# A sixth seven-product pair in the first halves of the down-projection's four-group parts, and more block sums kept in HBM

## The chip, the cores and the metric

The kernel runs on one core of a Trainium2 chip. The metric is the device time of one execution in microseconds (us); the time of a version is the median of its runs. TensorE multiplies matrices and accumulates in PSUM (eight banks of 128 x 512 float32). VectorE and ScalarE work element by element, GpSimd (POOL) does a little and issues some transfers, SyncE (SP) issues most transfers between HBM and the on-chip memory SBUF. The engines run side by side, each through its own instructions in their order, and wait for each other by semaphores.

## The reference

A decoder trunk of two layers on 256 tokens with a width of 2048. The first layer mixes tokens by a gated spatial product, the second by latent attention; both add attention into 256 memory tokens. Each layer ends with a gated feed-forward part with a causal convolution over three tokens. All is float32. The feed-forward part is what the change is about:

```python
def conv_ffn(h, w_up, cw, cb, w_down):
    S = h.shape[1]
    a = h @ w_up                                   # 256 x 2048 by 2048 x 11264
    ap = jnp.pad(a, ((0, 0), (CONV_W - 1, 0), (0, 0)))
    c = sum(ap[:, k:k + S] * cw[k] for k in range(CONV_W)) + cb
    gate, val = c[..., :D_FF], c[..., D_FF:]       # D_FF = 5632
    return (jax.nn.silu(gate) * val) @ w_down      # 256 x 5632 by 5632 x 2048
```

`out = rmsnorm(x + conv_ffn(rmsnorm(x)))` closes the second layer; the first hands `x` on to the next.

## The kernel before, in words

**Precision.** Each float32 operand is split in a rounded high half and the rest (`whi` and `wlo` for weights). A product is three matmuls: high by high, high by low, low by high. ScalarE writes the high half (L718 in the down-projection, L127 in the up-projection), VectorE the low half (L719, L128). Weights come through `raw` (four buffers of 512 KB) or `gate` (two) and go into `whi` (four) and `wlo` (five), so that loads and splits run ahead of TensorE.

**Parts.** The 11 groups of 512 hidden columns are worked in three parts of 4, 4 and 3 groups (`FF_GROUPS`). In a part, each group has an up-projection for the gate and one for the value, of eight chunks of weights each (`gemm_fm`). Each chunk is 24 matmuls of 256 columns. After the last chunk of an up-projection its four blocks of 128 hidden columns leave PSUM: `conv` multiplies by the row norm (L246, tile `a`, two buffers), then makes the three-tap convolution (L967 on ScalarE, L968 and L969 on VectorE, tile `c`, three buffers); `ev` multiplies by the gate (L989, or L996 and L1000) and splits the result as an operand of the down-projection (L254 and L255, or L1007 and L1008). Small jobs are hung on the chunks (`hooks`, by number of the chunk).

**The down-projection.** After its groups a part multiplies its 8 (or 6) pairs of 128-row blocks with the matching rows of `w_ffn_down`, first for the left 1024 output columns (half 0), then for the right (half 1). This is `down_phase`. A plain pair takes 2 blocks x 2 token halves x 2 column halves x 3 = 24 matmuls of 512 columns. A fast pair takes seven products of sums of blocks instead of eight (Strassen's way), 7 x 3 = 21 matmuls, into the accumulators e00, e01, e10 and m1, m5, m6, m7. For that the operand is kept in seven or eight quarters (`parts7`, made at L996 to L1008), and the weights need two tiles of sums beside the blocks themselves (`t13`, `t24`, four additions of 128 x 512). After the last fast pair of a half the four m accumulators are copied to `staged`; they are added to the result in the next part (`combine`).

**Where the sums come from.** There are three ways. Early sums (`FF_EARLY`): loaded and added in the last group's up-projections, for pairs 2 and 6 in a tile that shares its place (`xT`) with `staged`, for pair 5 in `xs` (two buffers). Stored sums (`FF_STORED`): long before, a hook loads 1 MB of the weights, adds, and POOL stores the sums in HBM (L792); the half loads them back into `xs`, or, for the one case named in `FF_STAGED`, into the free part of `staged`. Late sums (`late_sums`, L808): added on the spot. `FF_STORED` gives for each part (-1 is the output projection before) the hook's number, counted in chunks from the part's start, and the case (part, pair, half).

**Order.** `FF_FAST` gives for each half which pairs are fast and the order of all pairs. Loads on SP and splits on ScalarE and VectorE keep the program's order in `down_phase` (`behind`). Other instructions are put in order by the framework: each engine takes, by a simulated clock, the first instruction in program order that is ready. In half 0 of a four-group part the order is 0, 1, 5, 2, 7, 3, 6, 4, of which 2, 3, 4, 5, 6 are fast; pair 3's sums are stored, pair 4's late. The blocks of group g are 4g to 4g + 3 within the part, so pairs 6 and 7 come from the last group. What does not fit into the tile `h` goes to four `places` (tiles hx0 to hx3; other names in the last layer); a profile writes all of these as hhx.

Of the kernel before, what the change touches and what calls it, by code (L numbers as in the profile page):

```python
# [8 lines left out]
F32 = mybir.dt.float32  # L9
# [4 lines left out]
ALU = mybir.AluOpType  # L14
AX = mybir.AxisListType

P = 128
D = 2048
# [14 lines left out]
FF_GROUPS = (4, 4, 3)  # L33
FF_EARLY = {4: (2, 6, 5), 3: (1, 2, 4)}
FF_STORED = {
# [4 lines left out]
}  # L40
FF_STAGED = {4: (5, 1), 3: (5, 0)}
FF_FAST = {
    4: (((2, 3, 4, 6, 5), (0, 1, 5, 2, 7, 3, 6, 4)), ((2, 3, 4, 6, 5), (0, 2, 1, 3, 5, 4, 7, 6))),
    3: (((1, 2, 4, 5), (0, 3, 1, 2, 4, 5)), ((), (0, 1, 2, 3, 4, 5))),
}

# [35 lines left out]
class Kernel:  # L82
# [180 lines left out]
    def rstd(self, out, sums, n, pool, tag):  # L263
        nc = self.nc
        shape = list(out.shape)
        v = self.tmp(pool, shape, tag + "v", 1)
        r = self.tmp(pool, shape, tag + "r", 1)
        q = self.tmp(pool, shape, tag + "q", 1)
        nc.vector.tensor_scalar(v, sums, 1.0 / n, EPS, ALU.mult, ALU.add)
        nc.scalar.activation(r, v, AF.Sqrt)  # L270
        nc.vector.reciprocal(r, r)
        nc.vector.tensor_tensor(q, r, r, ALU.mult)
        nc.vector.scalar_tensor_tensor(q, q, -0.5, v, ALU.mult, ALU.mult)
        nc.vector.scalar_tensor_tensor(out, q, 1.5, r, ALU.add, ALU.mult)
# [487 lines left out]
    def stored_sums(self, l, case, pool):  # L762
        part, k, ph = case
        dn = self.t["w_ffn_down"][l][sum(FF_GROUPS[:part]) * 512 :]
        order = mybir.DependencyInfo(mybir.DependencyClass.NoSync, mybir.DependencyReason.DATA)
        add = lambda o, a, b: self.tc.keep_in_program_order(self.nc.vector.tensor_tensor(o, a, b, ALU.add))  # L766
        left, right, c = slice(0, 512), slice(512, 1024), 1024 * ph
        held = []

        def load(out, in_):  # L770
            ins = self.nc.sync.dma_start(out=out, in_=in_)
            self.tc.add_manual_dep(ins.ins, self.last_raw, order, reason="behind")

        def loads():
            held.extend(self.tmp(pool(), [P, 1024], "xs", 2) for _ in range(2))
            t13, t24 = held
            x, y = (dn[(2 * k + i) * P : (2 * k + i + 1) * P, c : c + 1024] for i in range(2))
            load(out=t13, in_=x)
            load(out=t24[:, left], in_=y[:, right])
            load(out=t24[:, right], in_=y[:, left])  # L780

        def adds():
            t13, t24 = held
            add(t13[:, left], t13[:, left], t13[:, right])
            add(t13[:, right], t13[:, right], t24[:, left])
            add(t24[:, left], t24[:, left], t13[:, left])
            add(t24[:, right], t24[:, right], t24[:, left])

        def stores():
            kept = self.stored[l, *case] = self.dram.tile([P, 2, 1024], F32, name=self.uid("stored"))  # L790
            for i in range(2):
                self.nc.gpsimd.dma_start(out=kept[:, i], in_=held[i])  # L792

        return loads, adds, stores

    def storing(self, l, part, pool):
        hooks = {}
        for n, case in FF_STORED[part].items():
            loads, adds, stores = self.stored_sums(l, case, pool)
            for m, f in (n, loads), (n + 5, adds), (n + 8, stores):  # L800
                hooks.setdefault(m // 8, {}).setdefault(m % 8, []).append(f)
        return hooks

    def late_sums(self, raws, pool):
# [29 lines left out]
    def down_phase(self, dn, col, order, fast, lhs, rhs, pool, fp, between, evict, finish, late=0, late_gains=None, hooks={}, sums={}, stored={}):  # L834
# [3 lines left out]
        left, right = slice(0, 512), slice(512, 1024)  # L838
# [4 lines left out]
        total = dict(todo)  # L843
# [15 lines left out]
        kept = []  # L859
        last_fast = [k for k in order if k in fast][-1:]  # L860
        for n, k in enumerate(order):
            raws = []
            for i in range(2):
                if n % 3 == (2 if col else 1) and n > 1:
                    raw = self.tmp(fp, [P, 1024], "gate", 2)
                else:
                    raw = self.wp.tile([P, 1024], F32, tag="raw", name=self.uid("raw"), bufs=4)
                raws.append(raw)
            kept_sums = stored.get((k, col // 1024))
            load = lambda o, a: self.behind(self.nc.sync.dma_start(out=o, in_=a))  # L870
            row = lambda i, c: load(raws[i][:, :c], dn[(2 * k + i) * P : (2 * k + i + 1) * P, col : col + c])
            blocks = sums.get(k)
            if kept_sums is None:
                row(0, 1024 if blocks is None else 512)
                row(1, 1024)
            else:
                if (k, col // 1024) == FF_STAGED[len(order) // 2]:
                    tile = self.tokens.staged[:, 1].rearrange("p m c -> p (m c)")
                    blocks = [tile[:, i * 1024 : (i + 1) * 1024] for i in range(2)]
                else:  # L880
                    blocks = [self.tmp(pool, [P, 1024], "xs", 2) for _ in range(2)]
                row(1, 1024)
                for i in (1, 0):
                    load(blocks[i], kept_sums[:, i])
                row(0, 512)
            if k in fast and blocks is None:
                blocks = self.late_sums(raws, pool)
            if late_gains is not None and 2 <= n:
                late_gains(n - 2)
            if k in fast:  # L890
                names7 = "e00", "e01", "e10", "m6", "m5", "m7", "m1"
                for name, q, w in zip(names7, (1, 6, 2, 5, 4, 3, 0), self.fast_pair(raws, blocks)):
                    three(name, rhs(k, q), w)
                if k in last_fast:
                    between([acc[m] for m in names[0]])
            else:
                ws = self.plain_pair(raws)
                if n < len(order) - late:
                    for tb in range(2):
                        for half in range(2):  # L900
                            plain(k, ws, tb, half)
                else:
                    kept.append((k, ws))
            for f in hooks.get(n, ()):
                f()
# [6 lines left out]
        with self.tc.manual_schedule(engines={ET.PE, ET.DVE, ET.Activation}):  # L912
# [9 lines left out]
            k, ws = kept[-1]  # L922
# [510 lines left out]


class Tokens:
    places = ("hx0", 0), ("hx1", 0), ("hx2", 0), ("hx3", 0)

    def __init__(self, kernel, pool):
        self.k, self.nc, self.pool = kernel, kernel.nc, pool
# [40 lines left out]
    def between(self, accs):  # L1480
        for i, acc in enumerate(accs):
            self.nc.scalar.activation(self.staged[:, self.ph, i, :], acc, AF.Copy)
        self.waiting.append(self.ph)
# [90 lines left out]


class Last(Tokens):
    places = ("kT1", 32), ("mv1", 0), ("hx", 0), ("hx3", 0)

    def __init__(self, kernel, pool):
        super().__init__(kernel, pool)  # L1580
# [19 lines left out]
    def evict(self, tb, half, acc, piece=None, meanwhile=lambda: None):  # L1600
        k, nc, xt, sums = self.k, self.nc, self.xt, self.sums
        c0, n = (0, 512) if piece is None else (256 * piece, 256)
        j, o = self.added(tb, half, acc, c0, n)
        c = slice(j * 512 + c0, j * 512 + c0 + n)
        if not self.last:
            return
        one = lambda x: x[:, tb : tb + 1]
        part, r, q, v, gb = self.part, self.r, self.q, self.v, self.gb
        junk = k.tmp(self.pool, [P, 512], "fjunk", 2)
        if piece == 1:  # L1610
            nc.vector.tensor_tensor_reduce(
                out=junk[:, :n], in0=o, in1=o, scale=-0.5 / D, scalar=one(part), op0=ALU.mult, op1=ALU.add, accum_out=one(v)
            )
        else:
            nc.scalar.activation(junk[:, :n], o, AF.Square, accum_out=sums[:, tb, j : j + 1])
        if piece == 0:
            self.added(tb, half, acc, 256, 256)
        meanwhile()
        if j < 3 and not (tb and j == 2):
            nc.vector.tensor_tensor(o, o, gb[:, c], ALU.mult)  # L1620
# [4 lines left out]
            if tb:  # L1625
                nc.vector.tensor_tensor(o, o, gb[:, c], ALU.mult)
        if j == 3:
            if piece != 1:
                total = one(part) if piece == 0 else one(v)
                nc.vector.tensor_scalar(total, sums[:, tb, 3:4], -0.5 / D, one(part), ALU.mult, ALU.add)  # L1630
            if piece == 0:
                return
            nc.scalar.activation(one(r), one(v), AF.Sqrt, scale=-2.0)
            nc.vector.reciprocal(one(r), one(r))
            nc.vector.scalar_tensor_tensor(one(q), one(r), one(r), one(v), ALU.mult, ALU.mult)
            nc.vector.scalar_tensor_tensor(one(r), one(q), 1.5, one(r), ALU.add, ALU.mult)
# [36 lines left out]
```

## Time and profile before

| | |
|---|---|
| median of 3 runs | 2022.09 us (2021.52 to 2022.26) |
| the profiled execution | 2022.45 us, its span 2020.7 us |
| TensorE busy | 2010.5 us (99%) |
| VectorE, ScalarE busy | 1665.6 us (82%), 1184.9 us (59%) |
| down-projection of the first part, layer 0 | 528.11 to 608.70 us |
| moved by DMA | 463.27 MB, 229 GB/s |

A row of a timeline has the start, the duration, the engine, the line of the kernel, the operation, the tiles written and read, the shape and the count; in brackets stands the idle time before it and what ended it. A row of windows has the stretch, its length, the busy time of TensorE, of its weight loads, of VectorE, ScalarE and POOL, the granted clock (1.00 is full), the share of the DMA engines and GB/s. Matmuls are pipelined, and each is shown longer than the distance to the next; so one reads distances between starts. The execution's time is longer than the span by what lies around the program.

### The profile page before, as it was taken

How to read it: one execution, taken by the hardware profiler on the slowest of the kernel's cores; microseconds unless marked ns; L12 is line 12 of the kernel's file. 1: busy time of each engine (PE TensorE's matmuls, PEld its weight loads, DVE VectorE, ACT ScalarE, POOL GpSimd, SP SyncE). 2: the span in 40 equal slices, each digit the busy share in tenths (PEclk: the TensorE clock that was granted, in tenths of full speed). 3: DMA queues.
4: the chain of work that ended last, by engine and by line, in shares of the span. 5: the costliest groups of instructions: out<-in, count | busy, mean ns of one | idle time of the engine just before them, and what ended most of it. 6: DMA issues, size and time to landing. Idle time of an engine off the chain costs nothing.

```text
span 2020.7 us, 38415 instructions
## 1 busy us (share of the span) xinstructions
PE 2010.5 (99%) x15098; PEld 1905.3 (94%) x15098; DVE 1665.6 (82%) x2519; ACT 1184.9 (59%) x1687; POOL 129.1 (6%) x205
## 2 busy tenths in 40 slices
PE   9999999999999999999999999999999999999998
PEld 8989999999989999899989999999988999889996
DVE  6866767788898788988988787778889878898897
ACT  6754744555665556655576675455566555665565
POOL 0000013100000000000002142400000000000000
PEclk9999999999999999999999999999999999999999
DMA  8775567888668786678566636788867878667865
GB/s 256 232 217 180 166 217 254 232 293 276 210 235 266 246 275 211 233 234 261 185 224 187 183 113 203 235 242 288 275 206 237 273 237 275 206 235 233 275 187 179
DMA packets 269897, 463.27 MB, mean 229 GB/s; under 512 B 77774, under 2 KB 85268, under 8 KB 269716
## 3 DMA queue, kind: packets, MB, share of 16 engines
q1 hardware_dynamic: 264340, 441.40, 68.6%
q0 software_dynamic: 5184, 18.88, 2.6%
q8 instruction: 118, 1.93, 0.4%
q14 instruction: 63, 0.52, 0.1%
q10 hardware_dynamic: 192, 0.54, 0.1%
HBM read 435.06 MB, written 20.97 MB: 226 GB/s over the span
## 4 chain that ended last, share of the span: by engine, by line
PE 98%; DVE 1%; ACT 1%; DMA 0%; issue 0%; SPq 0%; ACTq 0%; DVEq 0%
PE ps L166 22%; PE ps L167 22%; PE ps L169 22%; PE ps L850 7%; PE ps L851 7%; PE ps L852 7%; PE ps L198 2%; PE ps L199 2%; PE ps L200 2%; PE ps L533 1%; DMA raw<-in_w_ffn_down 0%; PE ps L613 0%; PE ps L612 0%; PE ps L611 0%; PE ps L415 0%; PE ps L1324 0%
## 5 line engine op out<-in xcount | busy, mean ns | idle before, releaser
L127 ACT ACTIVATE whi<-raw 128x1024 fp32r<-128x1024 f32 x484 | 513.7, 1062 | 528.7 <-PE ps L167 387.3
L128 DVE TENSOR_TENSOR wlo<-raw,whi 128x1024 fp32r<-128x1024 f32 x484 | 597.1, 1238 | 204.2 <-ACT whi L127 200.6
L166 PE MATMUL ps<-xhl,whi 128*128 128x256 f32 x3264 | 763.3, 277 | 0.0
L167 PE MATMUL ps<-xhl,whi 128*128 128x256 f32 x3264 | 761.6, 276 | 0.0
L167 PEld LDWEIGHTS ps<-xhl,whi 128*128 128x128 f32 x3264 | 612.8, 188 | 0.4
L166 PEld LDWEIGHTS ps<-xhl,whi 128*128 128x128 f32 x3264 | 612.8, 188 | 0.4
L169 PE MATMUL ps<-xhl,wlo 128*128 128x256 f32 x3264 | 438.0, 276 | 0.0
L169 PEld LDWEIGHTS ps<-xhl,wlo 128*128 128x128 f32 x3264 | 401.1, 188 | 0.0
L851 PE MATMUL ps<-wlo,h 128*128 128x512 f32 x354 | 137.1, 388 | 0.1
L719 DVE TENSOR_TENSOR wlo<-raw,whi 128x1024 fp32r<-128x1024 f32 x94 | 113.9, 1219 | 20.9 <-ACT whi L718 20.0
L718 ACT ACTIVATE whi<-raw 128x1024 fp32r<-128x1024 f32 x94 | 98.4, 1054 | 52.7 <-PE ps L167 32.2
L166 PE MATMUL ps<-mainhl,whi 128*128 128x256 f32 x512 | 119.7, 277 | 0.0
L167 PE MATMUL ps<-mainhl,whi 128*128 128x256 f32 x512 | 119.3, 276 | 0.0
L852 PE MATMUL ps<-whi,h 128*128 128x512 f32 (+1 forms) x306 | 118.4, 388 | 0.0
L967 ACT ACTIVATE c<-a,cT 128x256 f32<-128x256 f32 x176 | 99.0, 591 | 29.4 <-DVE a L246 28.4
L850 PE MATMUL ps<-whi,h 128*128 128x512 f32 x354 | 108.3, 389 | 0.0
L167 PEld LDWEIGHTS ps<-mainhl,whi 128*128 128x128 f32 x512 | 96.0, 188 | 0.0
L166 PEld LDWEIGHTS ps<-mainhl,whi 128*128 128x128 f32 x512 | 95.9, 188 | 0.0
L792 POOL DMA_DIRECT2D stored<-xs x36 | 19.8, 550 | 1158.9 <-DVE xs L766 985.1
L718 ACT ACTIVATE whi<-xs 128x1024 fp32r<-128x1024 f32 x60 | 62.7, 1058 | 47.6 <-DVE xs L808 23.7
L133 DVE SCALAR_TENSOR_TENSOR wlo<-raw,gT,whi 128x512 fp32r<-128x512 f32 x96 | 71.0, 779 | 21.3 <-ACT whi L132 21.2
L852 PE MATMUL ps<-whi,hhx 128*128 128x512 f32 x216 | 84.0, 389 | 0.0
(401 smaller groups left out, 3131.6 us busy)
## 6 DMA issues: line engine op xcount, KB each, us to landing
raw<-in_w_ffn_up SPq DMA_DIRECT2D x352, 512.0 KB, 4.6
raw<-in_w_ffn_down SPq DMA_DIRECT2D x102, 512.0 KB, 5.8
raw<-in_w_out SPq DMA_DIRECT2D x64, 512.0 KB, 4.4
raw<-in_w_in_a SPq DMA_DIRECT2D x56, 512.0 KB, 4.4
gate<-in_w_ffn_down SPq DMA_DIRECT2D x38, 512.0 KB, 5.0
stored<-xs POOLq DMA_DIRECT2D x36, 512.0 KB, 5.3
raw<-in_w_mem_kv SPq DMA_DIRECT2D x31, 512.0 KB, 3.6
xs<-in_w_ffn_down SPq DMA_DIRECT2D x24, 512.0 KB, 6.5
```

Of the source, the lines that this page charges most:

```text
L127: nc.scalar.activation(hi[:, :n], raw[:, :n], AF.Copy)
L128: nc.vector.tensor_tensor(lo[:, :n], raw[:, :n], hi[:, :n].bitcast(F32), ALU.subtract)
L133: nc.vector.scalar_tensor_tensor(lo[:, s], raw[:, s], gains[k], hi[:, s].bitcast(F32), ALU.mult, ALU.subtract)
L166: mm(acc[:, :S], wh, x[:, :S], start=first, stop=False)
L167: mm(acc[:, :S], wh, x[:, S:], start=False, stop=False)
L169: mm(acc[:, :S], wl, x[:, :S], start=False, stop=last)
L718: self.behind(self.nc.scalar.activation(hi, w, AF.Copy))
L719: self.behind(self.nc.vector.tensor_tensor(lo, w, hi.bitcast(F32), ALU.subtract))
L850: mm(o, xh, wh, start=start, stop=False)
L851: mm(o, xh, wl, start=False, stop=False)
L852: mm(o, xl, wh, start=False, stop=stop)
L967: nc.scalar.activation(c, a, AF.Identity, scale=w(2), bias=w(3))
```

## The change

In half 0 of the four-group parts pair 1 becomes the sixth fast pair, and pairs 4 and 1 have their sums stored ahead, as pair 3 has. That makes 13 stored cases in a layer where there were 9, 12 of them for four-group parts. The order of that half becomes 0, 7, 2, 6, 5, 3, 4, 1. Stored cases now start every eight chunks, and each is hung on the chunks in five pieces (two loads, the additions, two stores) at 0, 1, 5, 6 and 7 chunks from its start, where there were three pieces at 0, 5 and 8. Pair 3's stored sums come back into one half of `staged` and pair 1's into the other, pair 4's into `xs`. A fifth place is added for operands; to make room the row norm uses the `sq` buffers for two of its tiles. At the very end, the sum of squares of the last quarter is put together after the last addition and not before it.

```diff
 FF_STORED = {
-    -1: {8: (0, 2, 1), 20: (0, 5, 1)},
-    0: {17: (0, 3, 0), 28: (0, 4, 1), 39: (1, 3, 0)},
-    1: {8: (1, 2, 1), 22: (1, 5, 1), 36: (1, 4, 1)},
+    -1: {8: (0, 2, 1), 16: (0, 5, 1), 24: (0, 4, 1)},
+    0: {16: (0, 3, 0), 24: (0, 4, 0), 32: (0, 1, 0), 40: (1, 3, 0)},
+    1: {2: (1, 4, 0), 10: (1, 1, 0), 18: (1, 2, 1), 26: (1, 5, 1), 34: (1, 4, 1)},
     2: {20: (2, 5, 0)},
 }
-FF_STAGED = {4: (5, 1), 3: (5, 0)}
+FF_STAGED = {4: {(3, 0): 1, (1, 0): 0, (5, 1): 1}, 3: {(5, 0): 1}}
 FF_FAST = {
-    4: (((2, 3, 4, 6, 5), (0, 1, 5, 2, 7, 3, 6, 4)), ((2, 3, 4, 6, 5), (0, 2, 1, 3, 5, 4, 7, 6))),
+    4: (((2, 3, 4, 6, 5, 1), (0, 7, 2, 6, 5, 3, 4, 1)), ((2, 3, 4, 6, 5), (0, 2, 1, 3, 5, 4, 7, 6))),
     3: (((1, 2, 4, 5), (0, 3, 1, 2, 4, 5)), ((), (0, 1, 2, 3, 4, 5))),
 }
...
     def rstd(self, out, sums, n, pool, tag):
-        v = self.tmp(pool, shape, tag + "v", 1)
+        v, q = (self.tmp(pool, shape, *(("sq", 2) if tag == "rb" else (tag + x, 1))) for x in "vq")
         r = self.tmp(pool, shape, tag + "r", 1)
-        q = self.tmp(pool, shape, tag + "q", 1)
...
-        return loads, adds, stores
+        return [lambda: loads(0), lambda: loads(1), adds, lambda: stores(0), lambda: stores(1)]
 
     def storing(self, l, part, pool):
         hooks = {}
         for n, case in FF_STORED[part].items():
-            loads, adds, stores = self.stored_sums(l, case, pool)
-            for m, f in (n, loads), (n + 5, adds), (n + 8, stores):
-                hooks.setdefault(m // 8, {}).setdefault(m % 8, []).append(f)
+            for m, f in zip((0, 1, 5, 6, 7), self.stored_sums(l, case, pool)):
+                hooks.setdefault((n + m) // 8, {}).setdefault((n + m) % 8, []).append(f)
         return hooks
...
-                if (k, col // 1024) == FF_STAGED[len(order) // 2]:
-                    tile = self.tokens.staged[:, 1].rearrange("p m c -> p (m c)")
+                home = FF_STAGED[len(order) // 2].get((k, col // 1024))
+                if home is not None:
+                    tile = self.tokens.staged[:, home].rearrange("p m c -> p (m c)")
...
 class Tokens:
-    places = ("hx0", 0), ("hx1", 0), ("hx2", 0), ("hx3", 0)
+    places = ("hx0", 0), ("hx1", 0), ("hx2", 0), ("hx3", 0), ("hx4", 0)
...
 class Last(Tokens):
-    places = ("kT1", 32), ("mv1", 0), ("hx", 0), ("hx3", 0)
+    places = ("kT1", 32), ("mv1", 0), ("hx", 0), ("hx2", 0), ("hx3", 0)
...
         if piece == 1:
+            nc.vector.tensor_scalar(one(part), sums[:, tb, 3:4], -0.5 / D, one(part), ALU.mult, ALU.add)
             nc.vector.tensor_tensor_reduce(
...
         if piece == 0:
             self.added(tb, half, acc, 256, 256)
+            return
...
-            if piece != 1:
-                total = one(part) if piece == 0 else one(v)
-                nc.vector.tensor_scalar(total, sums[:, tb, 3:4], -0.5 / D, one(part), ALU.mult, ALU.add)
-            if piece == 0:
-                return
+            if piece is None:
+                nc.vector.tensor_scalar(one(v), sums[:, tb, 3:4], -0.5 / D, one(part), ALU.mult, ALU.add)
```

More of the change, by code (lines that the diff above doesn't have):

```diff
@@ L772, in load, with loads @@
             self.tc.add_manual_dep(ins.ins, self.last_raw, order, reason="behind")
[L774 to L780, printed above, removed]
+        def loads(i):
+            held.append(self.tmp(pool(), [P, 1024], "xs", 2))
+            w = dn[(2 * k + i) * P : (2 * k + i + 1) * P, c : c + 1024]
+            if i == 0:
+                load(out=held[0], in_=w)
+            else:
+                load(out=held[1][:, left], in_=w[:, right])
+                load(out=held[1][:, right], in_=w[:, left])
         def adds():
@@ L787, in adds, with stores @@
             add(t24[:, right], t24[:, right], t24[:, left])
[L789 to L792, printed above, removed]
-        return loads, adds, stores
+        def stores(i):
+            if i == 0:
+                self.stored[l, *case] = self.dram.tile([P, 2, 1024], F32, name=self.uid("stored"))
+            self.nc.gpsimd.dma_start(out=self.stored[l, *case][:, i], in_=held[i])
+        return [lambda: loads(0), lambda: loads(1), adds, lambda: stores(0), lambda: stores(1)]
     def storing(self, l, part, pool):
```

## The prediction

> **What bounds the kernel now.** I read the page first (busy time, the chain), then the waits of TensorE, then the down-projection stages by windows and by timeline.
>
> ```profile
> span 2020.7 us, 38415 instructions
> ...
> PE 2010.5 (99%) x15098; PEld 1905.3 (94%) x15098; DVE 1665.6 (82%) x2519; ACT 1184.9 (59%) x1687; POOL 129.1 (6%) x205
> ...
> PE 98%; DVE 1%; ACT 1%; DMA 0%; issue 0%; SPq 0%; ACTq 0%; DVEq 0%
> ...
> L166 PE MATMUL ps<-xhl,whi 128*128 128x256 f32 x3264 | 763.3, 277 | 0.0
> ```
>
> TensorE holds 98% of the chain and is idle 0.0 before its largest group: the time is the number of matmuls times their spacing, plus what little TensorE waits. So a removed matmul pays in full, and a new wait costs in full. Now one down-projection stage (chain of waits, timeline and windows; in the third row the operation is counted for line 851 alone):
>
> ```profile
> 528.11 0.40 PE L850 MATMUL ps<-whi,hhx 128*128 128x512 f32 x1
> 533.57 0.39 PE L850 MATMUL ps<-whi,hhx 128*128 128x512 f32 x1
> 528.11:608.70 80.59, 46.00 (x118) 22.15 (x118) 1.00 0.67 229
> 539.17 0.91 PE ps L850 x4
> 528.11:568.51 40.40, 40.40 (x179) 33.15 (x178) 36.71 (x52) 27.17 (x34) 0.00 (x0) 1.00 0.56 190
> 568.51:608.70 40.19, 40.19 (x178) 33.16 (x177) 36.86 (x41) 26.68 (x31) 0.00 (x0) 1.00 0.78 267
> ```
>
> Four matmuls of 512 columns take 0.91 us, 0.227 each. The stage has 3 x 118 = 354 of them, 80.4 us; it takes 80.6, so about 0.25 us is waiting. A plain pair is 24 matmuls (5.45 us: 528.11 to 533.57 is the first), a seven-product pair 21 (4.77 us).
>
> **Step 1, the products removed.** Pair 1 becomes a seven-product pair in the first half of four stages (two layers, two four-group parts): 4 x 3 = 12 matmuls of 0.227 us, **-2.7 us**. Nothing lies beside them: TensorE is the path.
>
> **Step 2, the late sums removed.** Pair 4 now forms its sums inside the stage. This is where it happens:
>
> ```profile
> 560.81 0.69 DVE L808 TENSOR_TENSOR xs<-gate,gate 128x512 f32<-128x512 f32 x1
> 561.41 1.41 DVE L808 TENSOR_TENSOR xs<-xs,gate 128x512 f32<-128x512 f32 x2
> 562.74 1.22 DVE L719 TENSOR_TENSOR wlo<-gate,whi 128x1024 fp32r<-128x1024 f32 x1
> 563.49 1.29 PE L850 MATMUL ps<-whi,h 128*128 128x512 f32 x4
> 564.62 0.40 PE L851 MATMUL ps<-wlo,h 128*128 128x512 f32 x1
> ```
>
> VectorE adds just before TensorE reaches the pair, and four matmuls there take 564.62 - 563.49 = 1.13 us instead of 0.91. With the sums read from HBM the 0.25 us of the stage should go: 4 stages, **-1.0 us**. The bounds: 0 (another wait takes its place) and -1.3.
>
> **Step 3, the new order, and a wait.** The first half now runs 0, 7, 2, 6, 5, 3, 4, 1 where it ran 0, 1, 5, 2, 7, 3, 6, 4. Pair 7 is blocks 14 and 15 of the part, the last two that the last up-projection writes; it moves from fifth to second place, so its first matmul is due at 533.57, not after 548. When is it ready? VectorE and ScalarE after the last up matmuls (the tile named hhx in L254 and L255 is pair 7):
>
> ```profile
> 527.62 0.75 DVE L246 TENSOR_TENSOR a<-ps,rbc 128x256 f32<-128x256 f32 x2 [0.63 <-PE ps L169]
> 528.54 1.23 DVE L719 TENSOR_TENSOR wlo<-raw,whi 128x1024 fp32r<-128x1024 f32 x1 [0.17 <-ACT whi L718]
> 530.48 0.87 DVE L969 SCALAR_TENSOR_TENSOR c<-a,cT,c 128x254 f32<-128x254 f32 x2
> 531.60 0.42 DVE L246 TENSOR_TENSOR a<-ps,rbc 128x256 f32<-128x256 f32 x1
> 532.27 0.41 DVE L246 TENSOR_TENSOR a<-ps,rbc 128x256 f32<-128x256 f32 x1
> 534.92 1.22 DVE L719 TENSOR_TENSOR wlo<-raw,whi 128x1024 fp32r<-128x1024 f32 x1
> 536.05 0.75 DVE L989 TENSOR_TENSOR gate<-gate,c 128x256 f32<-128x256 f32 x2
> 536.50 0.75 ACT L254 ACTIVATE hhx<-gate 128x256 fp32r<-128x256 f32 x2 [0.39 <-DVE gate L989]
> 536.73 1.21 DVE L719 TENSOR_TENSOR wlo<-xs,whi 128x1024 fp32r<-128x1024 f32 x1
> 537.86 1.08 DVE L1008 TENSOR_TENSOR h<-src,h 128x896 fp32r<-128x896 f32 x1
> 538.86 0.75 DVE L255 TENSOR_TENSOR hhx<-gate,hhx 128x256 fp32r<-128x256 f32 x2
> ```
>
> VectorE is at work all the while. The buffer `a` has two copies, so blocks 14 and 15 enter (531.60, 532.27) only when 12 and 13 have left the convolution (530.48 on). One operation of this size takes 0.41 or 0.42 (the single L246 rows), so the high half of block 14 is there at 536.50 + 0.42 = 536.92 and its low half at 538.86 + 0.41 = 539.27, block 15's about 0.35 later. Nothing in the edit touches these lines. The two weight splits between them (534.92, 536.73) belong to the third pair of the order; that pair is 2 instead of 5, but its buffers come free at the same time.
>
> TensorE can't go round pair 7. Products into one accumulator keep their order, as a stage elsewhere shows: four first products (one for each accumulator), then transposes of a later hook come ahead of the pair's other products.
>
> ```profile
> 1040.27 1.07 PE L850 MATMUL ps<-whi,hhx 128*128 128x512 f32 x4
> 1041.18 0.38 PE L415 MATMUL ps<-ident,xt 128*128 128x128 f32 x2
> ```
>
> So pair 2's products into e00, e01, e10 stay behind pair 7's; its m5 and m7 need a weight buffer that pair 7 holds (four of `whi`), its m1 the tile `src` that L1008 still reads. Only the three products of m6 may go ahead. Between 533.57 and 539.27 (5.70 us) TensorE can do 4 x 2 products of block 14 that need no low half, and those three: 11 x 0.227 = 2.5 us. Lost: 3.2 us; 3.9 without the three. Behind the waiting product on TensorE stand the other 150 of the half; ScalarE's split of pair 2's second sum waits with them for `whi`. After 539.27 all is ready and what follows is only shifted. I take 3.2, since products that are ready do go ahead, as those transposes did: 4 x 3.2 = **+12.8 us**; bounds +8.8 (below, half the wait) and +15.6.
>
> **Step 4, sums stored ahead: eight cases more** (pairs 4 and 1, four parts). Each: 3 loads on SP, 4 adds on VectorE, 2 stores on POOL, 2 loads back.
>
> ```profile
> stored<-xs POOLq DMA_DIRECT2D x36, 512.0 KB, 5.3
> xs<-stored SPq DMA_DIRECT2D x24, 512.0 KB, 6.5
> L766 DVE TENSOR_TENSOR xs<-xs,xs 128x512 f32<-128x512 f32 x36 | 24.7, 685 | 0.3
> L792 POOL DMA_DIRECT2D stored<-xs x36 | 19.8, 550 | 1158.9 <-DVE xs L766 985.1 <-DVE c L969 165.5 <-DMA raw<-in_w_out 4.2
> 353.50:527.99 174.49, 174.49 (x1539) 174.44 (x1539) 146.59 (x223) 96.26 (x124) 10.01 (x14) 1.00 0.83 258
> 585.00:595.00 10.00, 10.00 (x46) 8.29 (x45) 8.53 (x9) 7.27 (x9) 0.00 (x0) 1.00 0.91 311
> ACT whi L127 <- DMA raw<-in_w_ffn_up: 62.8, 40, 6.4
> ```
>
> Adds: 4 x 0.685 = 2.7 us a case. VectorE is busy 146.6 of 174.5 us in an up-projection; two cases more make 152: hidden. POOL issues in 0.55 us and is otherwise idle. Transfers: 1 MB in, 1 MB out and 0.75 MB more in the stage, 8 x 2.75 = 22 MB, some 240 GB/s instead of 229; the densest 10 us show 311 with TensorE full. In the stage a read-back must land between pair 6's last read of the shared tile and pair 3's use, 9 + 21 + 6 matmuls = 8.2 us apart, against 6.5 median; the second half has this pattern already and loses nothing (40.19). The finer cases stand every 8 chunks instead of 11 to 14: SP, in order, waits for a store to land before it loads into the same tile, and the up-projection's loads stand behind it. Today's late loads make ScalarE wait 6.4 us at the longest and TensorE 0.0, since splits run ahead. One more megabyte at 311 GB/s is 3.4 us. I take 0, bounds 0 and +3 (first part of layer 0, where SP also issues the transposes' transfers). Moved `v` and `q` of the row norm: no wait that the sums they follow don't have, 0.
>
> **Step 5, the end.** VectorE's last rows:
>
> ```profile
> 2012.06 0.75 DVE L1503 TENSOR_TENSOR xt<-ps,xt 128x256 f32<-128x256 f32 x2
> 2013.12 0.21 DVE L1630 TENSOR_SCALAR fpart<-fsums,fpart 128x1 f32<-128x1 f32 x1 [0.30 <-ACT fjunk L1615]
> 2013.25 0.41 DVE L1503 TENSOR_TENSOR xt<-ps,xt 128x256 f32<-128x256 f32 x1
> ```
>
> The addition at 2013.25 no longer stands behind the wait for ScalarE's square; it fills the 0.30 us of idle: **-0.3 us**, bounds 0 and -0.4.
>
> **Sum:** -2.7 - 1.0 + 12.8 + 0 - 0.3 = +8.8 us. The profiled execution is 2022.45 us (span 2020.7 and 1.75 around it), so 2031.3; it lies 0.36 above the median of the runs, 2022.09, and I forecast **2030.9 us** for the median.
>
> **Rivals.** A: pair 7's wait is not there (its blocks come first, or other work fills the place). For it: step 3 rests on one order of VectorE that is made anew when the program is built. Against it: nothing in the edit asks for another order. Then -2.7 - 1.0 - 0.3 = -4.0: 2018.1, faster. It decides when block 14's low half is ready by 534; every 0.33 us a stage later takes one third of the gain.
>
> B: half the wait. If VectorE and ScalarE take pair 7 ahead of the two splits (2 x 1.13 us between starts, 534.92 to 536.05), the low half is ready at 537.0; five products fill 1.2 of the 3.4 us, 2.2 us lost a stage: +8.8 - 4.0, 2026.9.
>
> C: the long waits slow the clock.
>
> ```profile
> 2012.30:2017.20 4.90, 0.00 (x1) 0.00 (x0) 3.24 (x11) 2.06 (x6) 0.00 (x0) 1.00 0.54 213
> 2017.30:2020.70 3.40, 0.00 (x0) 0.00 (x0) 0.00 (x0) 0.00 (x0) 0.00 (x0) 0.50 0.56 221
> ```
>
> After the last matmul the granted clock stays 1.00 for 4.9 us and is 0.50 then; my wait is 3.3 us, shorter, so I don't expect it. If it came, pair 7's 16 products left (3.6 us) would take twice that: 4 x 3.6 more, 2045. The Trainium skill, "TensorE: Matmul & The Clock Gate", section "What's actually happening", has the gate halve the clock after an idle window of about 3.4 us, free-running; by it a 3.3 us wait stays just under, and a slow window would cost half of 3.4 us a stage, 2037.7. The trace's 4.9 us at full clock agrees that the one window isn't always enough.
>
> D: loads starve an up-projection or pairs 3, 4, 1: step 4's +3 on top, 2034.
>
> **Chances.** Forecast 0.58 (own range 2028 to 2034), A 0.17, B 0.13, C 0.05, D 0.07. Range **2020 to 2036**: it leaves out most of A and C, 0.2. This measurement tells 0.2% (4.0 us) from no change. Faster than 2018.05 is about two thirds of A with a little luck elsewhere: 0.12. Within: the rest of A with a loss, and the low part of B: 0.16. Slower: 0.72.
>
> **What would show it.** The first half of each four-group stage at 42.7 us instead of 40.4 and the second at 40.1; idle time of TensorE after the stage's first 24 matmuls, put down to ScalarE's L254 or VectorE's L255 writing pair 7's tile; 12 matmuls fewer; VectorE's order before 539 as above. Step 2 is right if four matmuls at the half's end take 0.91. I am wrong if the first half takes 39.5 us: then A holds; idle TensorE in an up-projection would be D.

## The result and the profile after

The changed kernel takes **2038.95 us** (median) against 2022.17 us for the kernel before on the same chip: a ratio of 1.0083, 95% interval 1.0070 to 1.0097. It is slower by 16.8 us; 2030.9 was forecast, with a range up to 2036. Five of its six executions took 2038.5 to 2039.4 us; the sixth, slow one took 3412.7 us at a granted clock of 0.555 and is left out of the ratio. The profiled execution takes 2038.52 us, its span is 2036.8.

The page of the changed kernel (span, busy time, shares of the chain):

```profile
span 2036.8 us, 38592 instructions
...
PE 2015.2 (99%) x15086; PEld 1908.0 (94%) x15086; DVE 1680.4 (83%) x2551; ACT 1192.3 (59%) x1691; POOL 134.1 (7%) x221
...
PE 96%; DVE 2%; ACT 1%; DMA 0%; issue 0%; SPq 0%; ACTq 0%; DVEq 0%
```

Twelve matmuls are gone (15098 to 15086), and the span is 16.1 us longer. TensorE's share of the chain falls from 98% to 96%: it waits now. Its waits in the whole execution (us in total, number, longest):

```profile
PE ps L849 <- ACT whi L717: 6.4, 4, 1.6
PE ps L849 <- ACT hhx L254: 4.6, 4, 1.1
PE ps L499 <- DVE ones L296: 1.1, 1, 1.1
PE ps L849 <- ACT staged L1482: 0.6, 1, 0.6
```

Four stages, two waits in each (the view counts from the modelled end of a matmul; by distances between starts they are about 1.76 and 1.41 us). Before, TensorE had no wait over 0.2 us but the one of 1.1 at the start. The columns of the next view are stretch, length, busy time of TensorE, its weight loads, VectorE, ScalarE and POOL, granted clock, DMA share, GB/s. The rows are the first half of the first stage and its second half, the first half of the second stage, and the first halves of the two stages of layer 1:

```profile
528.49:574.14 45.65, 42.91 (x176) 34.65 (x175) 36.95 (x51) 28.64 (x36) 0.00 (x0) 0.93 0.60 216
574.14:614.26 40.12, 40.12 (x178) 33.22 (x177) 36.27 (x41) 27.07 (x31) 0.00 (x0) 1.00 0.77 266
788.36:831.30 42.94, 40.19 (x177) 32.43 (x175) 36.50 (x49) 28.24 (x35) 0.00 (x0) 1.00 0.64 226
...
1490.60:1534.84 44.24, 41.51 (x176) 33.71 (x175) 37.85 (x52) 29.07 (x36) 0.00 (x0) 0.96 0.63 223
1749.06:1793.42 44.36, 41.63 (x177) 33.76 (x176) 37.57 (x52) 29.28 (x36) 0.00 (x0) 0.96 0.61 223
```

The four first halves took 40.4 us each before, 161.6 in all; now they take 177.2, 15.6 more: nearly all of the loss. They differ, and the granted clock tells them apart. The half with a clock of 1.00 took 42.94; the three with 0.93 and 0.96 took 1.3 to 2.7 us more. Here is the place in the first stage (timeline: start, duration, and in brackets the idle time and what ended it):

```profile
533.73 0.39 PE L851 MATMUL ps<-whi,hhx 128*128 128x512 f32 x1
...
535.30 1.22 DVE L718 TENSOR_TENSOR wlo<-raw,whi 128x1024 fp32r<-128x1024 f32 x1
...
535.72 0.50 PE L849 MATMUL ps<-whi,h 128*128 128x512 f32 x1 [1.60 <-ACT whi L717]
...
536.89 0.75 ACT L254 ACTIVATE hhx<-gate 128x256 fp32r<-128x256 f32 x2 [0.39 <-DVE gate L989]
537.11 1.22 DVE L718 TENSOR_TENSOR wlo<-sums,whi 128x1024 fp32r<-128x1024 f32 x1
...
537.36 0.80 PE L849 MATMUL ps<-whi,hhx 128*128 128x512 f32 x1 [1.14 <-ACT hhx L254]
...
538.38 0.63 PE L849 MATMUL ps<-whi,hhx 128*128 128x512 f32 x1
538.81 0.63 PE L850 MATMUL ps<-wlo,hhx 128*128 128x512 f32 x1
...
539.25 0.75 DVE L255 TENSOR_TENSOR hhx<-gate,hhx 128x256 fp32r<-128x256 f32 x2
```

Pair 0 ends at 533.96 (533.73 + 0.227). One product of pair 2 (`h`) goes ahead at 535.72, pair 7 (`hhx`) begins at 537.36, when ScalarE has written block 14's high half (536.89 + 0.42 = 537.31). From 538.38 on the matmuls follow each other at 0.43 us instead of 0.227: half clock. The order of VectorE is that of before.

### The profile page after: what moved, and what is told of

Same layout as the page of the kernel before. It is cut to its first block, busy times and chain, and to the rows that moved or that the text cites. A ratio compares the mean times of both kernels' runs of the same rounds, so it can differ in the third digit from the quotient of the medians.

```text
span 2036.8 us, 38592 instructions
## 1 busy us (share of the span) xinstructions
PE 2015.2 (99%) x15086; PEld 1908.0 (94%) x15086; DVE 1680.4 (83%) x2551; ACT 1192.3 (59%) x1691; POOL 134.1 (7%) x221
## 4 chain that ended last, share of the span: by engine, by line
PE 96%; DVE 2%; ACT 1%; DMA 0%; issue 0%; SPq 0%; ACTq 0%; DVEq 0%
PE ps L166 22%; PE ps L167 22%; PE ps L169 22%; PE ps L850 7%; PE ps L849 7%; PE ps L851 7%; PE ps L198 2%; PE ps L199 2%; PE ps L200 2%; PE ps L532 1%; DVE wlo L718 1%; DMA raw<-in_w_ffn_down 0%; ACT whi L717 0%; PE ps L612 0%; PE ps L610 0%; PE ps L611 0%
## 5 line engine op out<-in xcount | busy, mean ns | idle before, releaser
L792 POOL DMA_DIRECT2D stored<-xs x52 | 28.3, 544 | 1169.9 <-DVE xs L765 1017.4
L851 PE MATMUL ps<-whi,hhx 128*128 128x512 f32 x240 | 92.1, 392 | 0.0
L849 PEld LDWEIGHTS ps<-whi,h 128*128 128x128 f32 x354 | 66.4, 188 | 21.7 <-ACT whi L717 8.2
```

The source lines that it names most:

```text
L849: mm(o, xh, wh, start=start, stop=False)
L851: mm(o, xl, wh, start=False, stop=stop)
```

## The experiments

**1. The order alone.** The kernel before, pairs 1 and 7 exchanged; no sixth fast pair, no more stored sums.

```diff
-    4: (((2, 3, 4, 6, 5), (0, 1, 5, 2, 7, 3, 6, 4)), ...
+    4: (((2, 3, 4, 6, 5), (0, 7, 5, 2, 1, 3, 6, 4)), ...
```

> Only the order of the kernel before is changed: pairs 1 and 7 of the first half change places (0, 7, 5, 2, 1, 3, 6, 4). Theory W (the new place of pair 7 costs a wait, and the wait the clock): TensorE stands still twice after the first 24 matmuls of each of the four stages, 1.76 and 1.42 us as in the changed kernel, 3.2 to 3.6 us a stage, and in some stages one or two stretches of 3.41 us at half clock follow, 0 to 2.7 us a stage; in all +13 to +20 us, 2035 to 2042 us, granted clock below 0.999. Theory S (the stored sums and their transfers are the cost, the order is not): no difference, 2021 to 2024 us.

2039.62 us, ratio 1.0089 (1.0074 to 1.0104). TensorE's waits are the same two, to the tenth:

```profile
PE ps L850 <- ACT whi L718: 6.4, 4, 1.6
PE ps L850 <- ACT hhx L254: 4.6, 4, 1.1
```

So the new place of pair 7 alone costs as much as the whole change, 17.6 us over the kernel before in the same measurement, and theory S falls. Two of the four first halves took 43.8 us at a clock of 1.00, 3.4 more than before; the second and the fourth took 45.3 and 45.2 at 0.96. In the changed kernel it was the first, the third and the fourth that lost their clock.

**2. Matmuls that nobody needs, first form.** 12 matmuls with pair 0's operands and weights, after pair 0.

```diff
+            if n == 0 and not col and len(order) == 8:
+                spare = self.psum()
+                for _ in range(12):
+                    mm(spare, lhs(0, 0)[0], ws[0][0][:, left], start=True, stop=True)
```

> The changed kernel with 12 unused matmuls of 512 columns (2.7 us) between pair 0 and pair 7 in the first half of the four stages; they write a spare bank that nobody reads. Theory W: they lie in the wait of 3.4 us, pair 7 begins no later, TensorE's busy share stays high, the clock stays at 1.00, and the 5.6 us that the half clock costs in the four stages are gone: 2033.4 us (2032 to 2035), granted clock 0.999. Rival (pair 7 runs slowly because its operands come late, not because of the clock): no gain, 2039 us. Rival (the 12 matmuls are simply more work): 4 x 2.7 us more, 2050 us.

2029.59 us: 9.4 us faster than the changed kernel with 10.9 us of useless work in it, and outside every expectation. The timeline shows why it can't price the clock: the wait itself is gone (L993 is L989 of the changed kernel, L907 the useless matmuls):

```profile
533.26 2.88 PE L907 MATMUL ps<-whi,hhx 128*128 128x512 f32 x12
...
534.61 0.42 DVE L993 TENSOR_TENSOR gate<-gate,c 128x256 f32<-128x256 f32 x1
534.95 1.22 DVE L718 TENSOR_TENSOR wlo<-raw,whi 128x1024 fp32r<-128x1024 f32 x1
535.27 0.40 ACT L254 ACTIVATE hhx<-gate 128x256 fp32r<-128x256 f32 x1
...
535.99 0.39 PE L849 MATMUL ps<-whi,hhx 128*128 128x512 f32 x1
...
536.18 1.07 ACT L717 ACTIVATE whi<-sums 128x1024 fp32r<-128x1024 f32 x1 [0.51 <-PE ps L907]
```

The useless matmuls hold a `whi` buffer, so pair 2's second split comes only at 536.18, and VectorE takes block 14 ahead of the first split; in experiment 3, where no weight buffer is held, the split stands ahead again. Block 14's high half is there at 535.67 (535.27 + 0.40), before the 12 matmuls end, and pair 7 runs with no wait. 2029.59 less 10.9 is 2018.7, an estimate of what the change is worth without wait and without half clock. The first half of its first stage, by windows:

```profile
527.80:570.02 42.22, 42.22 (x189) 34.87 (x187) 36.85 (x50) 28.59 (x36) 0.00 (x0) 1.00 0.66 227
```

186 matmuls at 0.227 us, and no wait. Block 14's high half comes 535.67 - 527.80 = 7.87 us after the stage's first matmul, in the changed kernel 8.82: the order of VectorE, which is settled when the program is built, moves it by 0.95 us.

**3. The same without holding a weight buffer.** Both operands are now pair 0's own (`block(0)`, a place that the profile writes as hhx); no weight buffer is read.

```diff
-                    mm(spare, lhs(0, 0)[0], ws[0][0][:, left], start=True, stop=True)
+                    mm(spare, lhs(0, 0)[0], self.filler, start=True, stop=True)   # filler is block(0)
```

> Again the changed kernel with 12 unused matmuls of 512 columns (2.7 us) after pair 0 in the first half of the four stages, but they read only operands in h, so that no weight buffer is held longer and the orders of VectorE and ScalarE up to pair 7 stay those of the changed kernel (block 14's high half 8.8 us after the stage's first matmul). Theory W: pair 7 begins no later, TensorE is busy in the wait, the clock stays at 1.00, and the 5.6 us of half clock are gone: 2033.4 us (2032 to 2035). Rival (pair 7's slow matmuls come from its late operands, the clock only shows it): 2037 to 2040 us. Rival (the useless matmuls are work on the path): 2044 to 2050 us.

2033.75 us, ratio 1.0058 (1.0043 to 1.0073): 48 more matmuls, 5.2 us faster than the changed kernel, in the range of theory W. The second and the fourth first half compare best, since pair 7 starts in them as late as in the changed kernel. There (windows) they took 42.94 at 1.00 and 44.36 at 0.96, here:

```profile
786.24:829.12 42.88, 42.59 (x189) 34.76 (x187) 37.76 (x52) 29.40 (x36) 0.00 (x0) 1.00 0.63 230
...
1746.71:1789.57 42.86, 42.57 (x189) 34.76 (x187) 36.36 (x50) 28.43 (x35) 0.00 (x0) 1.00 0.65 229
```

In the fourth 1.5 us is what the half clock had cost. The second, which had kept its clock, gains nothing (42.94 and 42.88). The first and the third took 43.61 and 44.07, both at 1.00: pair 7 begins in them 0.7 and 1.2 us later than in the changed kernel, and without that they would have taken 42.9 too. In both, VectorE has two weight splits ahead of L246 of blocks 12 and 13, which comes 0.4 and 1.0 us after the stage's first matmul; in the changed kernel it comes 0.5 us before. So this form too moved the order of VectorE, in two stages. The splits in the first stage (L246 follows at 528.82):

```profile
526.54 2.36 DVE L718 TENSOR_TENSOR wlo<-raw,whi 128x1024 fp32r<-128x1024 f32 x2 [0.36 <-ACT whi L717]
```

The four first halves are 3.8 us shorter than in the changed kernel, and the wait of 0.6 for `staged` is gone as well. That the total came out at theory W's 2033.4 is in part luck; that the clock stays and what it costs is shown by the second and the fourth half.

**4. VectorE takes pair 7's operand ahead of pair 2's splits.**

```diff
+            if n == 2 and not col and len(order) == 8:
+                for ins in self.ended:        # the last L254 and L255
+                    self.behind(ins)
             if k in fast:
```

> The changed kernel, and on VectorE and ScalarE the weight splits of pair 2 are put behind the operations that write pair 7's operand (L254, L255). Theory W in the form of rival B of the prediction (what stands ahead of pair 7's operand on VectorE is the two splits, 2 x 1.2 us): block 14's high half comes about 1.2 us earlier, its low half 2 us earlier, one stretch of idle of 1.6 to 2.4 us a stage is left, and the clock stays at 1.00: 2026 to 2029.5 us. Rival (the blocks' own path from the last up-projection matmul through the convolution is as long as the wait): no gain in the wait, 2033 to 2039 us.

2031.93 us, slower than expected (2026 to 2029.5). One wait is left in each stage:

```profile
PE ps L849 <- ACT hhx L254: 9.1, 4, 2.5
```

By distances between starts it is 2.4 to 2.7 us, where 1.6 to 2.4 was expected: the blocks' own way through the convolution is most of the 3.5. What was not expected either is that the clock still halves in two of the four stages.

**5 and 6. Pair 2 second, pair 7 third.** In the second form the second pair of an order doesn't use `src` (`own` at n == 1, in every half).

```diff
-    4: (((2, 3, 4, 6, 5, 1), (0, 7, 2, 6, 5, 3, 4, 1)), ...
+    4: (((2, 3, 4, 6, 5, 1), (0, 2, 7, 6, 5, 3, 4, 1)), ...
```
```diff
+        if own:
+            b11 = self.split_tile("whi", True)[:, left], self.split_tile("wlo", True)[:, left]
+        else:
             one = self.one or self.tmp(self.tokens.pool, [P, 1024], "src", 1, F32R)
```

> The changed kernel with pairs 7 and 2 in each other's places (0, 2, 7, 6, 5, 3, 4, 1). Without any wait the four first halves would take 39.45 us each instead of 45.65, 42.94, 44.24 and 44.36, 19.4 us less: 2019.5 us. Theory W: pair 7 (due after 538.7) finds its operands ready to within 1 us, but pair 2's last product m1 needs the tile src, which VectorE's L1008 reads until 539.3, and the splits of pair 7 stand behind the split into src in the order of the splits: 1.5 to 3 us a stage are lost, and the clock stays at 1.00: 2025 to 2032 us. Rival (the split order doesn't matter, only pair 7's own operands): 2019 to 2021 us.

> As the run before it (order 0, 2, 7, 6, 5, 3, 4, 1), and the second pair keeps the halves of its last weight block in whi and wlo buffers of its own instead of the tile src. If src is what holds pair 2 and the splits behind it (theory W), the wait falls to 0 to 1.5 us a stage, what VectorE still lacks: 2019 to 2026 us. If it isn't src but VectorE's backlog alone, no difference from the run before.

2030.7 us (1.0048, 1.0032 to 1.0063) and 2024.54 us (1.0014, 1.0004 to 1.0023), both with the clock at 0.999 in the profile. The first waits for `src`, as said:

```profile
PE ps L849 <- ACT src L717: 3.6, 5, 1.1
```

The second waits for VectorE, 2.8 us in all over the profile:

```profile
PE ps L853 <- DVE wlo L718: 1.7, 5, 0.6
...
PE ps L854 <- DVE hhx L255: 1.1, 4, 0.3
```

**7, 8 and 9. Pair 7 fast and last.** Pair 7 is the sixth fast pair in place of pair 1, with its sums stored ahead as pair 1's were. Nothing of pair 7 that the last up-projection writes is due early. `own` is the form of experiment 6, at the places named and in these halves alone.

```diff
-    4: (((2, 3, 4, 6, 5, 1), (0, 7, 2, 6, 5, 3, 4, 1)), ...
+    4: (((2, 3, 4, 6, 5, 7), (0, 1, 5, 2, 6, 3, 4, 7)), ...   # run 7, own at n == 2
+    4: (((2, 3, 4, 6, 5, 7), (0, 1, 2, 6, 5, 3, 4, 7)), ...   # run 8, own at n == 2; run 9, own at n in (2, 3)
```

> The changed kernel with another choice of the sixth fast pair: 7 instead of 1, with its sums stored ahead in the same way, and worked last: 0, 1, 5, 2, 6, 3, 4, 7; the third pair keeps the halves of its last weight block in whi and wlo buffers of its own. As many products, stored sums and transfers as in the changed kernel, but nothing that the last up-projection writes is due early. Theory W (place of pair 7 and clock explain all of the loss): first halves of 39.5 us as the matmuls give, 2019.5 us (2018.5 to 2021.5), clock 0.999. Rival S (the eight more stored cases or their transfers cost time of their own, up to 3 us): 2021.5 to 2023.5 us. Rival V (VectorE has more to do for pair 7's operand just when the half begins, 1.2 us and more, and the splits of the third and fourth pair come late): 1 to 3 us a stage, 2023.5 to 2031 us.

2043.13 us, slower than the change itself, and no theory had it. TensorE's longest wait, over the whole execution:

```profile
PE ps L852 <- ACT whi L717: 8.4, 4, 2.3
```

The longest wait of ScalarE between 545 and 565 us:

```profile
ACT whi L717 <- DMA staged<-stored: 4.9, 1, 4.9
```

The longest of SP's queue between 540 and 565 us:

```profile
SPq L872 <- DVE wlo L718: 12.4, 2, 12.2
```

They name the cause. Pair 3's sums come back into the tile that pair 6's sums share. In this order pair 3 follows pair 6 directly, SP issues the load only when VectorE has split pair 6's last sum, and the transfer lies open: TensorE waits 2.3 us at the longest, and the clock halves in three stages. The error was in my order, not in the stored sums. With pair 5 between them:

> As the run all_but_7second (sixth fast pair 7, worked last), with the order 0, 1, 2, 6, 5, 3, 4, 7: pair 5 stands between pairs 6 and 3, as in the changed kernel. If the 2.1 to 2.5 us before pair 3 (and the 0.7 and 0.37 behind them, and the half clock that three stages had) come from the stored sums, whose load waits for pair 6's last read of the shared tile, they are gone; what stays is VectorE's and src's lateness at pairs 2 and 6 and at the last pair, 0.5 to 1.2 us a stage: 2021.5 to 2024.5 us, clock 0.999. If the gap is VectorE's backlog, it moves to another pair: 2028 to 2042 us.

2025.39 us (1.0018, 1.0009 to 1.0026), a little above the range expected; the clock is at 0.999 and TensorE's wait for `whi` is 0.6 us in all, so the gap was the transfer. The profiled execution (2028.12 us, above the median) still shows 0.9 us of waits for `wlo` and 1.3 for `src`.

> As 7last_5between, and the fourth pair too keeps the halves of its last weight block in whi and wlo buffers of its own instead of src. If it is src (held by pair 7's operand until it is written) that makes the fourth pair late, 0.3 to 0.5 us a stage less than 7last_5between: 2019.5 to 2023 us. If the buffers of whi, now all four in use, are the next limit, as slow or slower: 2022 to 2030 us.

2020.91 us, ratio 0.9995 (0.9986 to 1.0004). The first half of the first stage in its profile (an execution of 2019.39 us), by windows; the other three took 39.55 or 39.56:

```profile
528.01:567.57 39.56, 39.56 (x177) 32.59 (x175) 37.71 (x52) 28.63 (x35) 0.00 (x0) 1.00 0.73 257
```

174 matmuls at 0.227 us are 39.5: the sixth fast pair gives its full gain where nothing waits. The median is 1.2 us below that of before, which this measurement can't tell from no change.

**10. The late sums alone.** Five fast pairs and the order of before; pair 4 stored, the finer pieces, the new end; pair 3's sums come back into `xs` as before.

```diff
-    4: (((2, 3, 4, 6, 5, 1), (0, 7, 2, 6, 5, 3, 4, 1)), ...
+    4: (((2, 3, 4, 6, 5), (0, 1, 5, 2, 7, 3, 6, 4)), ...      # without the cases (0, 1, 0) and (1, 1, 0)
```

> The kernel before with its five fast pairs and its order, and with the rest of the change: pair 4's sums are stored ahead (four cases more, in the finer pieces at every eight chunks), the end as changed. The step of the late sums: the 0.25 us that each first half loses at pair 4 go, 4 x 0.25 = 1.0 us, the end gives 0 to 0.3: 2021.0 us (2020.5 to 2021.5). Rival S (stored cases cost time): 2022 to 2025 us, with TensorE idle in an up-projection or before pair 4.

2020.88 us (0.9996, 0.9987 to 1.0005), and in the profile each first half is shorter by the 0.25 us that step 2 named (40.40 before):

```profile
527.94:568.09 40.15, 40.15 (x180) 33.23 (x179) 36.11 (x50) 27.93 (x35) 0.00 (x0) 1.00 0.67 223
```

## Why the prediction was wrong

The direction and the wait were right. The step that failed is what the wait brings with it: the half clock, rival C, was put at nothing, and it cost 5.4 us. The sum went from +8.8 to +16.1 us in the profile.

**Steps 1 and 2** (-2.7 and -1.0) hold: 12 matmuls fewer, the 0.25 us of the late sums gone (experiment 10), and 39.55 us for a first half without waits (experiment 9), where step 1 and 2 give 40.4 - 0.68 - 0.25 = 39.47.

**Step 3, the wait**, holds in place, cause and nearly in size. Block 14's high half was said to be ready 8.81 us after the stage's first matmul and is ready at 537.31, 8.82 after 528.49; the low half 11.16, now 539.67, 11.18. The second stage, which kept its clock, shows what TensorE did meanwhile:

```profile
793.60 0.39 PE L851 MATMUL ps<-whi,hhx 128*128 128x512 f32 x1
...
799.18 0.40 PE L850 MATMUL ps<-wlo,h 128*128 128x512 f32 x1
799.41 0.40 PE L851 MATMUL ps<-whi,h 128*128 128x512 f32 x1
799.65 0.43 PE L851 MATMUL ps<-whi,hhx 128*128 128x512 f32 x1
```

Pair 0 ends at 793.83 (793.60 + 0.227), and pair 7's first product with a low half begins at 799.65. Between them lie the eleven products of the sum: one of m6 ahead of pair 7, pair 7's eight, then m6's other two (`h`), which need the low half of pair 2's sum. So 5.82 us less 11 x 0.227 are lost, **3.3 us** where 3.2 was said. The whole first half was said to take 42.7 and takes 42.94, which is 3.5 over the 39.47 of steps 1 and 2; where the other 0.15 lie stays open. Counted with them, four stages are 13.9 instead of 12.8.

**Rival C is where it failed.** "My wait is 3.3 us, shorter, so I don't expect it" compared the wait with the 4.9 us of full clock after the last matmul, and C got a chance of 0.05. The clock halved in three of four stages; against 42.94 they took 2.71, 1.30 and 1.42 us more, **5.4 us** in all. Experiment 3, which keeps TensorE busy, holds the clock at 1.00 in all four and gives the 1.5 us of the fourth back. The row couldn't carry the conclusion drawn from it. Cut at multiples of 3.413 us back from the fall at 2017.28 (the grid of the last section), the same stretch of the kernel before reads:

```profile
2010.45:2013.86 3.41, 1.85 (x14) 1.57 (x12) 3.04 (x10) 2.38 (x7) 0.00 (x0) 1.00 0.62 240
2013.86:2017.27 3.41, 0.00 (x0) 0.00 (x0) 2.02 (x7) 1.54 (x3) 0.00 (x0) 1.00 0.39 150
```

The 4.9 us are the idle rest of a window in which TensorE had been busy for 1.85 us, and one whole idle window, at whose end the clock fell. So one idle window was enough there, and the 4.9 us are no idle time that is safe everywhere. C's price (3.6 us in each stage) was too high, since the half clock lasts one or two windows of 3.41 us, part of which was still idle. The Trainium skill, "TensorE: Matmul & The Clock Gate", section "What's actually happening", gave windows of that length. The estimate worked out from it, 2037.7, came nearest of all, in part by luck: it put 1.7 us into each of four stages, and by the same rule a wait of 3.3 us should have cost nothing.

**Step 4** (0) holds: the waits shown above are all that TensorE has over 0.2 us, and none is in an up-projection. Experiments 9 and 10 carry eight and four more cases without a loss. But the read-back has its bounds: with one pair less between the shared tile's last read and its next use it is the longest wait (experiment 7).

**Step 5** (-0.3) is -0.3 for the additions and less at the end:

```profile
2028.06 1.28 DVE L1503 TENSOR_TENSOR xt<-ps,xt 128x256 f32<-128x256 f32 x3
2029.26 0.20 DVE L1611 TENSOR_SCALAR fpart<-fsums,fpart 128x1 f32<-128x1 f32 x1
```

The three additions end 1.28 us after the first began (before 2013.66 - 2012.06 = 1.60), but the small operation that stood between them now stands behind them, 0.20: some 0.1 to 0.2 us are left.

**The sum again:** -2.7 - 1.0 + 13.9 + 5.4 - 0.2 = +15.4. The other 0.7 are about 0.4 that the first stage begins later (528.49, before 528.11) and 0.4 in the wait for `staged` (0.6 instead of 0.2); both are there or not from kernel to kernel, and their cause stays open.

Rival A is refuted by the waits. Rival B's mechanism was tried in experiment 4: putting pair 7 ahead of the splits leaves 2.4 to 2.7 us of wait, near the 2.2 it was priced at, but B too would have paid with the clock. Rival D has no wait to show for it.

## What to carry to other kernels

When work is reordered, ask for each operand when its producer is done, not only whether the buffers suffice; the one the previous stage writes last belongs behind work that is ready. A wait of a few microseconds on TensorE can have a second price in the granted clock after it, as here in three stages of four, so a forecast wait of that size needs two terms. Filling the place paid here even with useless work, and one has to see whether the filler changes the order of other engines, by a buffer that it holds or otherwise.

## What was not expected of the hardware

**The clock is decided in fixed windows, and a partly busy window can halve it.** Windows of 3.41 us of the changed kernel (the same columns):

```profile
533.28:536.69 3.41, 1.34 (x5) 0.56 (x3) 3.41 (x9) 3.22 (x4) 0.00 (x0) 1.00 0.18 70
536.69:540.11 3.42, 2.75 (x7) 2.17 (x8) 3.31 (x6) 0.75 (x2) 0.00 (x0) 0.50 0.00 0
540.11:543.52 3.41, 3.41 (x10) 2.64 (x9) 0.00 (x0) 0.00 (x0) 0.00 (x0) 0.50 0.68 215
...
792.69:796.11 3.42, 1.79 (x7) 0.94 (x5) 3.42 (x9) 3.36 (x5) 0.00 (x0) 1.00 0.30 116
...
1495.84:1499.25 3.41, 0.89 (x3) 0.19 (x1) 3.41 (x10) 3.02 (x5) 0.00 (x0) 1.00 0.09 35
1499.25:1502.66 3.41, 3.20 (x8) 2.56 (x9) 2.85 (x5) 0.49 (x2) 0.00 (x0) 0.50 0.02 5
1755.25:1758.66 3.41, 1.25 (x4) 0.85 (x5) 3.41 (x7) 2.57 (x5) 0.00 (x0) 1.00 0.00 0
```

The clock fell at 536.69, 1499.25 and 1758.66, which lie 962.56 and 259.41 us apart, 282 and 76 times 3.413: one grid through the whole execution. TensorE was busy for 1.34, 0.89 and 1.25 us of the window that ended there. The second stage, with the same two waits, lies otherwise on the grid; its window has 1.79, and the clock stays. The other kernels agree. From experiment 4, a window at the end of which it fell and one at which it stayed:

```profile
533.66:537.07 3.41, 1.32 (x6) 1.10 (x7) 3.41 (x9) 2.63 (x5) 0.00 (x0) 1.00 0.04 16
...
789.66:793.07 3.41, 1.68 (x8) 1.06 (x6) 3.41 (x11) 2.03 (x3) 0.00 (x0) 1.00 0.44 145
```

And from experiment 7 the busiest window that still ended in a fall:

```profile
1777.55:1780.97 3.42, 1.49 (x7) 0.91 (x6) 0.35 (x1) 1.25 (x2) 0.00 (x0) 1.00 0.97 357
```

In these runs the line lies between 1.49 and 1.68 us of busy time in 3.41, as the profile shows busy time, with modelled ends. So a wait of 2.4 us can be enough (experiment 4), and two shorter waits with a matmul between them too; which of four equal waits is punished depends on where it falls on the grid. After a fall the clock came back when a window had been full or nearly so (3.20 us at 1499.25); in the window from 536.69 TensorE was busy for 2.75 us, and a second slow one followed. The Trainium skill, "TensorE: Matmul & The Clock Gate", section "What's actually happening", has the free-running window of 3413 ns, which the grid confirms; it asks for an idle window of about that length, and there the traces differ: windows that were busy for up to 1.49 us were enough.
